# A chunked RWKV-7 recurrence: three chunk inverses side by side on half PSUM banks, their small levels as packed 32x32 squares

## The chip, the cores and the metric

The kernel runs on one core of a Trainium2 chip. TensorE (PE) multiplies into PSUM (8 banks of 128 partitions x 512 fp32), VectorE (DVE) and ScalarE (ACT) read PSUM, GpSimd (POOL) works on SBUF alone, and SyncE (SP) issues most DMAs. The metric is the device time of one execution in microseconds.

## The reference

A decoder trunk of two layers, for one prompt of 16 + 512 positions and eight sample rows of one position, all in fp32. Each layer is `x += ½ FFN(norm x)`, `x += Mixer(norm x)`, `x += ½ FFN(norm x)`. The even layer's mixer has four HGRN2 heads beside eight RWKV-7 heads, the odd layer's has GLA heads. The change touches the RWKV-7 part:

```python
def step(s, inp):                       # rwkv7_scan, per position and head (64 x 64 state)
    rt, wt, kt, vt, kkt, at = inp
    sa = jnp.einsum('bhij,bhj->bhi', s, -kkt)
    s = s * wt[:, :, None, :] + sa[..., None] * (kkt * at)[:, :, None, :] + vt[..., None] * kt[:, :, None, :]
    y = jnp.einsum('bhij,bhj->bhi', s, rt)
    return s, y
...
yn = ((y - mu) * lax.rsqrt(var + RWKV_GN_EPS)).reshape(bsz, t, B_W) * prm['rwkv_ln_w'][e] + prm['rwkv_ln_b'][e]
ob = (yn + bonus.reshape(bsz, t, B_W)) * g
mix = jnp.concatenate([oa.astype(f32), ob], axis=-1).astype(h.dtype) @ prm['even_w_out'][e]
```

## The kernel before

The prompt is cut into one chunk of 16 positions and eight of 64 (`CHUNKS`). Heads go in pairs on 128 partitions, and two such pairs make a group `d`; so there are 2 groups x 9 chunks = 18 units. In a unit the positions of a chunk are coupled by a triangular system, whose inverse is built by doubling: `stage_g` makes the products and the level for blocks of 1, then `lev_t` and `lev_x` for blocks of 2, 4, ... up to half the chunk. `xx` holds the inverse and its transpose, `gm` the masked products, `tm` transposed operands; all three exist for two head pairs side by side. Because the two heads of a pair and two halves of 32 positions lie apart, every level up to 16 is block-diagonal in 32x32 squares, but the kernel before multiplies the full 128x128. The state's update of a unit then goes through `st_p`, `st_t`, `st_sa`, `st_s` and `st_y`, in which PE and a copy or add take turns. `waves` puts all these steps into numbered slots, group 1 later than group 0 by `LAG`, and yields after each step.

`even_mixer` writes out the order of PE by hand (`manual_schedule` for PE; the other engines are ordered by the planner). After each step of the waves it spends a credit, raised by `FILL`, on other work in this order: the HGRN thread `hgrn` (`hproj`, projections in steps of 3 x 272 or 3 x 264 columns, and `hcore`, the recurrence of an HGRN head with `gla_core` and `gla_step`; a core step is charged 2500, for the last head 1000), and, when that is done, the output mix `mix_out` of the first 272 positions. Every `SAMPLE_EVERY` steps it calls the thread of the four RWKV sample states (`rsample`, one after the other; five transposes on PE, then DMA broadcasts, GpSimd products and two reductions; 16 yields each), every `POST_EVERY` steps `post`. `post` goes through the spans of `SPANS`; it starts none until the fourth head's projections are done (`while 3 not in H`), first drains what is left of the sample threads, makes the HGRN norm (`hgrn_norm`) as soon as the HGRN thread is done, and runs `rpost` for two head pairs at a time. The mix may begin when the norm and the spans up to 272 are done. `rsample`, `hgrn_norm` and `rpost` share the two scratch tiles `acc` and `sq`, one buffer each. After the waves:

```python
            now[0] = 10
            for _ in th_:
                pass
            for _ in po:
                if "first" in now and "half" in now:
                    credit = MIX
                    while credit > 0:
                        credit -= next(mo, credit)
            for _ in mo:
                pass
```

PSUM is given out in this stage as rings of whole banks: two for projections (`d`), two of `m` (HGRN cores, sample threads), four of `w` (waves and posts). The lines of the rows below: L240 to L242 projections and mix, L627 and L618 scores of the HGRN cores, L658 their product on GpSimd, L724 and L713 a core's first and last product, L1069 to L1117 the sample thread, L1159 to L1171 `stage_g`, L1182 to L1190 `lev_t`, L1204 and L1206 `lev_x`, L1222 and L1224 `st_p`, L1246 to L1261 `st_s` and `st_y`, L155 with `w` and L1314 to L1328 `rpost`, L176 to L180 and L866 to L869 the HGRN norm.

Of the kernel before, what the change touches and what calls it, by code (L numbers as in the profile page):

```python
# [51 lines left out]
NVEC = _r  # L52


FILL, FILL_MAX = 1100, 5000
CORE, CORE_LAST = 2500, 1000
BESIDE = 2000
AHEAD = 12864
POST = 2000
MIX = 4500  # L60

SAMPLE_EVERY, POST_EVERY = 3, 3
SPANS = [0, 272, 400, 536]
LAG, LAG_LATER = 2, 3
SMALL_BLOCK = 32

HEAD_EVERY, ODD_FILL = 5, 4000
# [2 lines left out]
CU_R, CU_G, CU_END = 0, 6 * 256, 6 * 256 + 6 * 32  # L70
# [36 lines left out]
def trunk(ctx, tc, A, O):  # L107
    nc = tc.nc
    P = 128
    cnt = [0]  # L110

    def til(pool, shape, tag, dt=F32, bufs=None):
        cnt[0] += 1
        kw = {} if bufs is None else {"bufs": bufs}
        return pool.tile(shape, dt, tag=tag, name=f"{tag}_{cnt[0]}", **kw)
# [5 lines left out]
    rings = {}  # L121
    banks = ctx.enter_context(ExitStack())

    def psum(**sizes):
        if sizes == {tag: n for tag, (_, n) in rings.items()}:
            return
        banks.close()
        rings.clear()
        for tag, n in sizes.items():
            pool = banks.enter_context(tc.tile_pool(name=f"ps{tag}", bufs=n, space=bass.MemoryType.PSUM))  # L130
            rings[tag] = (pool, n)

    def bank(tag="m"):
        return til(rings[tag][0], [P, 512], tag)


    cf = til(cst, [P, CF_RM], "cf")
# [983 lines left out]
    def waves(pool, R):  # L1121
# [9 lines left out]
        def lmask(li):  # L1131
            return cu[:, CU_R + 256 * li:CU_R + 256 * li + 256].unsqueeze(1).to_broadcast([P, 2, 256])

        def stage_g(d, ci, U):
            t0, n = CHUNKS[ci]
            na, nl = (2, 32) if n == 64 else (1, n)

            def both(z):  # L1140
                return z.rearrange("p (a h l) -> p a h l", a=2, h=2)[:, :na, :, :nl]

            U["xx"] = til(pool, [P, 2, 256], "xx", bufs=3)
            U["gm"] = til(pool, [P, 2, 320], "gm", bufs=3)
            nc.scalar.copy(U["xx"].rearrange("p u (v c) -> p (u v) c", v=2), ident.unsqueeze(1).to_broadcast([P, 4, P]))
            U["tm"] = til(pool, [P, 2, 384], "tm", bufs=3)
            if n < 64:
                nc.gpsimd.memset(U["gm"], 0.0)
            for i in range(2):
                Q = R[2 * d + i]  # L1150
                b_ = bd[i]
                for h in range(2):
                    hs = slice(64 * h, 64 * h + 64)
                    dst = b_[hs].rearrange("p (v a h l) -> p v a h l", v=4, a=2, h=2)[:, :, :na, h, :nl]
                    nc.vector.tensor_copy(dst, Q["sl"][hs, 0:4, t0:t0 + n].rearrange("p v (a l) -> p v a l", l=nl))
                g = bank("w")
                gv = g[:, 128:384].rearrange("p (v w t) -> p v w t", v=2, w=2)
                rhs = Q["sl"][:, 3:5, t0:t0 + n]
                nc.tensor.matmul(g[:, 0:128], b_[:, 384:512], b_[:, 0:128], start=True, stop=True)  # L1159
                nc.tensor.matmul(gv[:, 0, :, :n], b_[:, 0:128], rhs, start=True, stop=True)  # L1160
                nc.tensor.matmul(gv[:, 1, :, :n], b_[:, 128:256], rhs, start=True, stop=True)
                one = g[:, 128:128 + n].rearrange("p (a l) -> p a l", l=nl)
                nc.vector.tensor_mul(both(U["gm"][:, i, 0:128]), one.unsqueeze(2).to_broadcast([P, na, 2, nl]),
                                     both(maskg[:, 0:128]))
                nc.vector.copy_predicated(U["xx"][:, i, 0:128], cu[:, CU_R:CU_R + 128], g[:, 0:128])
                nc.vector.tensor_mul(*(z.rearrange("p (v t) -> p v t", v=3)[:, :, :n]
                                       for z in (U["gm"][:, i, 128:320], g[:, 192:384], maskg[:, 128:320])))
                pt = bank("w")
                for v in range(3):
                    nc.tensor.transpose(pt[:, 128 * v:128 * v + 128], b_[:, 128 * v:128 * v + 128], ident)  # L1170
                nc.scalar.copy(U["tm"][:, i], pt[:, :384])  # L1171
            nc.vector.copy_predicated(U["xx"][:, :, 128:256], lmask(0)[:, :, 128:256], U["gm"][:, :, 0:128])


        def lev_t(U, li):
            pt = bank("w")
            U["t1"] = til(pool, [P, 2, P], "t1", bufs=2)

            rs, cs = (slice(64, 128), slice(0, 64)) if li == 5 else (slice(0, 128), slice(0, 128))
            ks = cs  # L1180
            for i in range(2):
                nc.tensor.matmul(pt[rs, 128 * i:128 * i + cs.stop], U["gm"][ks, i, rs], U["xx"][ks, i, cs],  # L1182
                                 start=True, stop=True)
            if li > 1:
                px = bank("w")
                for i in range(2):
                    nc.tensor.transpose(px[:, 128 * i:128 * i + 128], U["xx"][:, i, 0:128], ident)  # L1187
            nc.scalar.copy(U["t1"][rs, :, cs], pt[rs, 0:256].rearrange("p (u c) -> p u c", u=2)[:, :, cs])
            if li > 1:
                nc.scalar.copy(U["xx"][:, :, 128:256], px[:, 0:256].rearrange("p (u c) -> p u c", u=2))  # L1190

        def lev_x(U, li, last):
            pd = bank("w")[:, 0:256].rearrange("p (u c) -> p u c", u=2)
            xx, t1 = U["xx"], U["t1"]
            if li == 5:
                a, b = slice(0, 64), slice(64, 128)
                for i in range(2):
                    nc.tensor.matmul(pd[a, i, a], t1[b, i, a], xx[b, i, 192:256], start=True, stop=True)
                nc.vector.tensor_copy(xx[a, :, 192:256], pd[a, :, a])
                return  # L1200
            for i in range(2):
                xt = xx[:, i, 128:256]
                lhsT, rhs = (t1[:, i], xt) if last else (xt, t1[:, i])
                nc.tensor.matmul(pd[:, i], lhsT, rhs, start=True, stop=True)  # L1204
            sl = slice(128, 256) if last else slice(0, 128)
            nc.vector.copy_predicated(xx[:, :, sl], lmask(li)[:, :, sl], pd)  # L1206


        def st_p(d, ci, U):
# [16 lines left out]
        def st_t(d, ci, U):  # L1226
            pt = bank("w")
            for i in range(2):
                nc.tensor.transpose(pt[:, 128 * i:128 * i + 128], pd[d][:, i], ident)
            U["pp"] = til(pool, [P, 2, P], "pp", bufs=2)  # L1230
            nc.scalar.copy(U["pp"], pt[:, 0:256].rearrange("p (u c) -> p u c", u=2))

        def st_sa(d, ci, U):
            ps = bank("w")
            for i in range(2):
                nc.tensor.matmul(ps[:, 128 * i:128 * i + 128], U["xx"][:, i, 128:256], U["pp"][:, i],
                                 start=True, stop=True)
            U["sa"] = til(pool, [P, 2, P], "sa", bufs=2)
            nc.scalar.copy(U["sa"], ps[:, 0:256].rearrange("p (u c) -> p u c", u=2))

        def st_s(d, ci, U):
# [26 lines left out]
        def inverse(d, w, U):  # L1268
            nl = 6 if CHUNKS[w][1] == 64 else 4
            yield lambda: stage_g(d, w, U)  # L1270
            for li in range(1, nl):
                yield lambda li=li: lev_t(U, li)
                yield lambda li=li: lev_x(U, li, li == nl - 1)

        slots = {}
        for d in range(2):
            t = LAG * d
            for w in range(9):
                U = {}
                for fn in inverse(d, w, U):  # L1280
                    slots.setdefault(t, []).append((1 + d, fn, 0))
                    t += 1
                if w == 0 and d == 1:
                    t += LAG_LATER
                for i, st in enumerate((st_p, st_t, st_sa, st_s, st_y)):
                    fn = lambda st=st, d=d, w=w, U=U: st(d, w, U)
                    slots.setdefault(t + i, []).append((0, fn, int(i == 4)))
        ends = 0
        for t in sorted(slots):
            for _, fn, end in sorted(slots[t], key=lambda z: z[0]):  # L1290
# [3 lines left out]
        for d in range(2):  # L1294
            for i in range(2):
                p = 2 * d + i
                ps = bank("w")
                nc.tensor.transpose(ps[:, :P], S[d][:, i], ident)
                so = til(pool, [P, 64], "so", bufs=2)
# [393 lines left out]
```

## Time and profile before

| | |
|---|---|
| median of 3 runs | 2305.53 us (2305.34 to 2306.35) |
| the profiled execution, its own time | 2313.27 us |
| its span from the first to the last instruction | 2311.5 us |
| PE busy | 2256.8 us, 98% |
| VectorE, ScalarE, GpSimd busy | 71%, 47%, 6% |
| PE's granted clock, mean | 0.991 of 2.4 GHz |

Matmuls overlap in PE's pipeline: the duration of one instruction is its way through the array, and what one costs is read from the distance of starts. An fp32 product is two instructions, a transpose is one.

### The profile page before, as it was taken

To read this page: it belongs to the slowest core of one execution; us is meant where nothing else is said; L and a number is where in the kernel's file an instruction comes from. 1 tells how busy PE (TensorE), PEld (TensorE's weight loads), DVE (VectorE), ACT (ScalarE), POOL (GpSimd) and SP (SyncE) were. 2 spreads that over 40 slices of the span, in tenths; PEclk is the share of its full clock that TensorE was granted. 3 is DMA by queue.
4 is the path that set the end of the run, shared out by engine and by line. 5 is a ranking of instruction groups with operands and counts; after the bars stand their busy time and mean duration, and the time that the engine had idled before them with its cause. 6 is when DMAs were issued, how large, how long until landed. Compare 5 with 4: busy or idle time off the path is not lost.

```text
span 2311.5 us, 47443 instructions
## 1 busy us (share of the span) xinstructions
PE 2256.8 (98%) x19520; PEld 2206.5 (95%) x19520; DVE 1646.7 (71%) x2971; ACT 1082.8 (47%) x2056; POOL 143.5 (6%) x192
## 2 busy tenths in 40 slices
PE   8999999999999999999999999999999999999998
PEld 8999999998998888999999999999999889999998
DVE  7858576686666878966757885857666777948576
ACT  6525254374444456434535452525434464525355
POOL 0000000312212100000000000000021210000000
PEclk9999999999999999999999999999999999999999
DMA  6323334223222116242423332333434353333324
GB/s 171 106 78 101 92 92 132 81 64 94 79 71 72 49 49 167 74 119 75 118 74 101 92 110 74 101 92 94 128 110 128 111 160 92 92 92 101 110 85 136
DMA packets 409393, 229.23 MB, mean 99 GB/s; under 512 B 19252, under 2 KB 400501, under 8 KB 409176
## 3 DMA queue, kind: packets, MB, share of 16 engines
q1 hardware_dynamic: 408456, 224.78, 33.5%
q8 instruction: 153, 2.51, 0.5%
q10 hardware_dynamic: 720, 1.42, 0.2%
q14 instruction: 64, 0.52, 0.1%
HBM read 211.19 MB, written 14.97 MB: 98 GB/s over the span
## 4 chain that ended last, share of the span: by engine, by line
PE 86%; DVE 5%; DMA 3%; ACT 2%; issue 1%; POOL 1%; SPq 0%; ACTq 0%; POOLq 0%; DVEq 0%
PE d L334 21%; PE d L335 21%; PE d L336 21%; PE d L240 5%; PE d L242 4%; PE d L241 4%; PE w L1182 1%; PE w L1204 1%; DMA vb<-dv 1%; DVE wlo L229 1%; DMA raw<-in_even_w_out_dram 1%; PE m L155 1%; DMA sq<-dr 1%; DMA raw<-in_odd_w_out_dram 1%; PE w L1187 1%
## 5 line engine op out<-in xcount | busy, mean ns | idle before, releaser
L240 PE MATMUL d<-hh,whi 128*128 128x264 f32 (+2 forms) x1136 | 343.6, 303 | 2.0 <-DVE xT L596 1.3
L242 PE MATMUL d<-hh,wlo 128*128 128x264 f32 (+2 forms) x1136 | 326.7, 288 | 1.9 <-DVE wlo L229 1.7
L241 PE MATMUL d<-hl,whi 128*128 128x264 f32 (+2 forms) x1136 | 326.6, 288 | 0.5 <-DVE hl L1418 0.5
L334 PE MATMUL d<-hh,whi 128*128 128x268 f32 (+1 forms) x832 | 237.8, 286 | 1.8 <-ACT hh L187 1.3
L335 PE MATMUL d<-hl,whi 128*128 128x268 f32 (+1 forms) x832 | 238.1, 286 | 0.9 <-DVE hl L188 0.9
L336 PE MATMUL d<-hh,wlo 128*128 128x268 f32 (+1 forms) x832 | 237.7, 286 | 0.7 <-DVE wlo L293 0.7
L240 PEld LDWEIGHTS d<-hh,whi 128*128 128x128 f32 x1136 | 216.1, 190 | 7.5 <-issue 2.4
L242 PEld LDWEIGHTS d<-hh,wlo 128*128 128x128 f32 x1136 | 215.4, 190 | 4.6 <-DVE wlo L229 4.0
L241 PEld LDWEIGHTS d<-hl,whi 128*128 128x128 f32 x1136 | 216.3, 190 | 0.9 <-DVE hl L1418 0.7
L534 DVE SCALAR_TENSOR_TENSOR xT<-d,xT 128x272 f32<-128x272 f32 (+2 forms) x192 | 82.9, 433 | 166.7 <-PE d L336 166.6
L334 PE MATMUL d<-hid,whi 128*128 128x264 f32 (+2 forms) x704 | 201.5, 287 | 0.0
L334 PE MATMUL d<-hid,whix 128*128 128x264 f32 (+2 forms) x704 | 201.2, 286 | 0.0
L335 PE MATMUL d<-hid,whix 128*128 128x264 f32 (+2 forms) x704 | 200.8, 285 | 0.0
L335 PE MATMUL d<-hid,whi 128*128 128x264 f32 (+2 forms) x704 | 200.7, 286 | 0.0
L336 PE MATMUL d<-hid,wlox 128*128 128x264 f32 (+2 forms) x704 | 200.6, 285 | 0.0
L336 PE MATMUL d<-hid,wlo 128*128 128x264 f32 (+2 forms) x704 | 200.5, 286 | 0.0
L334 PE MATMUL d<-sumh,whix 128*128 128x268 f32 (+1 forms) x576 | 170.9, 297 | 0.0
L336 PE MATMUL d<-sumh,wlo 128*128 128x268 f32 (+1 forms) x576 | 164.7, 286 | 0.0
L335 PE MATMUL d<-suml,whix 128*128 128x268 f32 (+1 forms) x576 | 164.4, 285 | 0.0
L334 PE MATMUL d<-sumh,whi 128*128 128x268 f32 (+1 forms) x576 | 164.2, 285 | 0.0
L336 PE MATMUL d<-sumh,wlox 128*128 128x268 f32 (+1 forms) x576 | 164.0, 285 | 0.0
L335 PE MATMUL d<-suml,whi 128*128 128x268 f32 (+1 forms) x576 | 164.0, 285 | 0.0
(383 smaller groups left out, 6557.8 us busy)
## 6 DMA issues: line engine op xcount, KB each, us to landing
raw<-in_ffn_gate_dram SPq DMA_DIRECT2D x44, 512.0 KB
raw<-in_ffn_up_dram SPq DMA_DIRECT2D x44, 512.0 KB
rawx<-in_ffn_gate_dram SPq DMA_DIRECT2D x44, 512.0 KB
rawx<-in_ffn_up_dram SPq DMA_DIRECT2D x44, 512.0 KB
raw<-in_ffn_down_dram SPq DMA_DIRECT2D x32, 512.0 KB
rawx<-in_ffn_down_dram SPq DMA_DIRECT2D x32, 512.0 KB
raw<-in_even_w_in_dram SPq DMA_DIRECT2D x30, 512.0 KB
raw<-in_odd_w_in_dram SPq DMA_DIRECT2D x25, 512.0 KB
```

The source lines that it names most:

```text
L155: nc.tensor.matmul(ps[:, :b - a], lhsT, rhs[:, a:b], start=True, stop=True)
L229: nc.vector.tensor_sub(lo[:, ks], raw[:, ks], hi[:, ks].bitcast(F32))
L240: nc.tensor.matmul(o, hi[:, k], h, start=(k == 0), stop=False)
L241: nc.tensor.matmul(o, hi[:, k], l, start=False, stop=False)
L242: nc.tensor.matmul(o, lo[:, k], h, start=False, stop=(k == nk - 1))
L334: nc.tensor.matmul(o, hi[:, k], rh(k), start=start and k == 0, stop=False, **kw)
L335: nc.tensor.matmul(o, hi[:, k], rl(k), start=False, stop=False, **kw)
L336: nc.tensor.matmul(o, lo[:, k], rh(k), start=False, stop=stop and k == nk - 1, **kw)
L534: nc.vector.scalar_tensor_tensor(xv[:, sl], ps, -0.5, xv[:, sl], ALU.mult, ALU.add)
L1182: nc.tensor.matmul(pt[rs, 128 * i:128 * i + cs.stop], U["gm"][ks, i, rs], U["xx"][ks, i, cs], start=True, stop=True)
L1187: nc.tensor.transpose(px[:, 128 * i:128 * i + 128], U["xx"][:, i, 0:128], ident)
L1204: nc.tensor.matmul(pd[:, i], lhsT, rhs, start=True, stop=True)
```

## The change

Three inverses run side by side in place of two, each stage of one every third slot (`CHAINS`, `STAGGER`), with the state's steps two slots apart (`OUT_STEP`). A `w` bank is given out as two halves of 256 columns, one after the other. Levels below the last one multiply the four diagonal 32x32 squares of each head pair (`squares_mm`), and `into` spreads the packed result over the masked places of `xx`. In `stage_g` the triangle is made as strips of 32 partitions into the unused part of a bank half, for both head pairs together. The post spans become four, since a half bank holds at most 256 columns. `FILL` falls from 1100 to 550, `SAMPLE_EVERY` goes from 3 to 6, `POST_EVERY` from 3 to 5. `xx`, `gm` and `tm` get four buffers, `pp`, `sa` and `so` one.

```diff
-FILL, FILL_MAX = 1100, 5000
+FILL, FILL_MAX = 550, 5000
...
-SAMPLE_EVERY, POST_EVERY = 3, 3
-SPANS = [0, 272, 400, 536]
-LAG, LAG_LATER = 2, 3
+SAMPLE_EVERY, POST_EVERY = 6, 5
+SPANS = [0, 144, 272, 400, 536]
+CHAINS, STAGGER, OUT_STEP = 3, 4, 2
...
     def bank(tag="m"):
-        return til(rings[tag][0], [P, 512], tag)
+        if tag != "w":
+            return til(rings[tag][0], [P, 512], tag)
+        if not halves:
+            t = til(rings[tag][0], [P, 512], tag)
+            halves.extend((t[:, 256:512], t[:, 0:256]))
+        return halves.pop()
...
-                g = bank("w")
-                gv = g[:, 128:384].rearrange("p (v w t) -> p v w t", v=2, w=2)
+                g, gl = bank("w"), bank("w")
+                gv = g.rearrange("p (v w t) -> p v w t", v=2, w=2)
                 rhs = Q["sl"][:, 3:5, t0:t0 + n]
-                nc.tensor.matmul(g[:, 0:128], b_[:, 384:512], b_[:, 0:128], start=True, stop=True)
+                lt = gl if i == 0 else lt
+                for a in range(na):
+                    for h in range(2):
+                        q = 64 * a + 32 * h
+                        nc.tensor.matmul(lt[q:q + 32, 32 * i:32 * i + nl], b_[:, 384 + q:416 + q],
+                                         Q["sl"][:, 0, t0 + 32 * a:t0 + 32 * a + nl], start=True, stop=True)
...
-                nc.vector.copy_predicated(U["xx"][:, i, 0:128], cu[:, CU_R:CU_R + 128], g[:, 0:128])
...
+                nc.tensor.transpose(gl[:, 128:256], b_[:, 0:128], ident)
                 pt = bank("w")
-                for v in range(3):
-                    nc.tensor.transpose(pt[:, 128 * v:128 * v + 128], b_[:, 128 * v:128 * v + 128], ident)
-                nc.scalar.copy(U["tm"][:, i], pt[:, :384])
+                for v in range(2):
+                    nc.tensor.transpose(pt[:, 128 * v:128 * v + 128], b_[:, 128 * v + 128:128 * v + 256], ident)
+                nc.scalar.copy(U["tm"][:, i, 0:128], gl[:, 128:256])
+                nc.scalar.copy(U["tm"][:, i, 128:384], pt)
+            into(U, 0, lt, 64 * na, nl)
...
+        def into(U, li, ps, rows, nl):
+            src = ps[:rows, 0:64].rearrange("p (u c) -> p u c", u=2)[:, :, :nl]
+            mk = cu[:rows, CU_R + 256 * li:CU_R + 256 * li + 128].rearrange("p (b c) -> p b c", b=4)
+            xx = U["xx"][:rows, :, 0:128].rearrange("p u (b c) -> p u b c", b=4)
+            nc.vector.copy_predicated(xx[:, :, :, :nl], mk.unsqueeze(1).to_broadcast([rows, 2, 4, 32])[:, :, :, :nl],
+                                      src.unsqueeze(2).to_broadcast([rows, 2, 4, nl]))
+        def squares_mm(ps, lhs, rhs):
+            for i in range(2):
+                for q in range(0, P, 32):
+                    nc.tensor.matmul(ps[q:q + 32, 32 * i:32 * i + 32], lhs[:, i, q:q + 32], rhs(i, q),
+                                     start=True, stop=True)
...
+                U["t1"] = til(pool, [P, 2, 32], "t1c", bufs=CHAINS)
+                squares_mm(pt, U["gm"], lambda i, q: U["xx"][:, i, q:q + 32])
...
+            if not last:
+                squares_mm(ps, xx[:, :, 128:256], lambda i, q: t1[:, i])
+                into(U, li, ps, P, 32)
+                return
...
+        free = [STAGGER * i for i in range(CHAINS)]
+        after, ends = [0, 0], []
+        for c in range(18):
+            d, w, U = c % 2, c // 2, {}
+            k = free.index(min(free))
+            t = max(free[k], ends[c - CHAINS - 1] if c > CHAINS else 0)
+            for fn in inverse(d, w, U):
+                slots.setdefault(t, []).append((1 + k, fn, 0))
+                t += CHAINS
+            free[k] = t
+            t = max(t - CHAINS + 2, after[d])
+            for i, st in enumerate((st_p, st_t, st_sa, st_s, st_y)):
+                fn = lambda st=st, d=d, w=w, U=U: st(d, w, U)
+                slots.setdefault(t + OUT_STEP * i, []).append((0, fn, int(i == 4)))
+            after[d] = t + 4 * OUT_STEP
+            ends.append(after[d])
```

## Rows read from the trace of the kernel before

**Rows 1.** The page: busy time by engine, and the chain that ended last.
```profile
PE 2256.8 (98%) x19520; PEld 2206.5 (95%) x19520; DVE 1646.7 (71%) x2971; ACT 1082.8 (47%) x2056; POOL 143.5 (6%) x192
...
PE 86%; DVE 5%; DMA 3%; ACT 2%; issue 1%; POOL 1%; SPq 0%; ACTq 0%; POOLq 0%; DVEq 0%
```
**Rows 2.** Windows of the stage: stretch, length, busy us by engine (instructions), PE clock, DMA.
```profile
520.30:868.70 348.40, 328.69 (x3406) 306.97 (x3405) 243.82 (x708) 160.92 (x437) 68.82 (x72) 0.98 0.24 69
868.70:889.80 21.10, 20.43 (x163) 20.19 (x164) 16.73 (x45) 10.51 (x29) 0.00 (x0) 1.00 0.43 121
```
**Rows 3.** Timeline of PE (start us, us, what): the fourth head's core begins and ends.
```profile
777.51 0.27 PE L724 MATMUL m<-cf,hv 128*8 128x128 f32 x1
...
816.39 0.39 PE L713 MATMUL m<-hq,S 128*128 128x128 f32 x2
```
**Rows 4.** Timeline: the fourth sample thread's first transposes, first GpSimd product, last reduction.
```profile
699.64 0.27 PE L1069 MATMUL m<-cf,sl 128*8 128x128 f32 x1
...
716.36 1.47 POOL L1091 TENSOR_TENSOR sq<-acc,sq 128x512 f32<-128x512 f32 x1
...
742.09 0.69 DVE L1117 TENSOR_REDUCE sl<-sq 128x8 f32<-128x512 f32 x1 [2.40 <-POOL sq L1115]
```
**Rows 5.** Timeline of PE: full products, and a step of projection between two of them.
```profile
645.99 0.39 PE L1246 MATMUL w<-tm 128*128 128x128 f32 x2
...
646.88 0.61 PE L1204 MATMUL w<-t,xx 128*128 128x128 f32 x4
647.25 0.37 PE L240 MATMUL d<-hh,whi 128*128 128x272 f32 x1
...
647.71 0.61 PE L1182 MATMUL w<-xx,gm 128*128 128x128 f32 x4
```
**Rows 6.** Timeline of PE: 32-wide score products, 64x64 products, and what follows each.
```profile
549.75 0.46 PE L627 MATMUL m<-hq,hk 128*32 128x32 f32 x32
550.14 0.38 PE L1236 MATMUL w<-pp,xx 128*128 128x128 f32 x1
...
653.45 0.44 PE L1198 MATMUL w<-xx,t 64*64 64x64 f32 x4
653.82 0.39 PE L240 MATMUL d<-hh,whi 128*128 128x264 f32 x1
```
**Rows 7.** Groups by line and form, PE, 520.3 to 868.7: count | busy us, mean ns | idle before.
```profile
L1182 PE MATMUL w<-xx,gm 128*128 128x128 f32 x280 | 45.0, 284 | 1.9 <-DVE xx L1206 1.9
L1204 PE MATMUL w<-t,xx 128*128 128x128 f32 x272 | 43.2, 283 | 1.3 <-ACT xx L1190 0.6 <-ACT t L1188 0.5
```
**Rows 8.** Groups by line and form, VectorE and ScalarE, 510 to 875: readers of `w`.
```profile
L1206 DVE COPY_PREDICATED xx<-cu,w 128x256 f32<-128x256 uint8 x70 | 30.5, 439 | 19.0 <-PE w L1204 18.4
...
L1166 DVE TENSOR_TENSOR gm<-w,cf 128x192 f32<-128x192 f32 x32 | 11.1, 347 | 0.0
...
L1163 DVE TENSOR_TENSOR gm<-w,cf 128x128 f32<-128x128 f32 x32 | 9.1, 284 | 4.6 <-PE w L1161 4.2
...
L1239 ACT COPY sa<-w 128x256 f32<-128x256 f32 x18 | 6.7, 373 | 4.6 <-PE w L1236 4.4
```
**Rows 9.** The same view: two engines that read one bank in `st_p`.
```profile
L1222 DVE COPY pd<-w 64x128 f32<-64x128 f32 x18 | 5.3, 295 | 13.0 <-ACT pd L1222 12.8
...
L1224 ACT COPY py<-w 128x128 f32<-128x128 f32 x18 | 4.7, 262 | 6.3 <-DVE pd L1222 6.3
```
**Rows 10.** The same view, GpSimd: a core's level.
```profile
L658 POOL TENSOR_TENSOR hk<-hk,dlev 128x264 f32<-128x264 f32 x12 | 10.8, 898 | 20.6 <-PE m L638 12.2 <-issue 8.0 <-POOL vb L750 0.4
```
**Rows 11.** Timeline: the norm's first and last work, a pair of posts' first and last.
```profile
828.30 0.65 ACT L176 ACTIVATE acc<-oa 128x536 f32<-128x536 f32 x1 [0.43 <-DVE hl L1328]
...
846.74 0.77 DVE L869 SCALAR_TENSOR_TENSOR hl<-oa,vcol,hh 128x536 fp32r<-128x536 f32 x1
...
868.30 0.29 DVE L1314 SCALAR_TENSOR_TENSOR acc<-w,sl 128x136 f32<-128x136 f32 x1
...
877.19 0.30 DVE L1328 TENSOR_TENSOR hl<-sq,hh 128x136 fp32r<-128x136 f32 x1 [0.16 <-ACT hh L1327]
```

More of the change, by code (lines that the diff above doesn't have):

```diff
@@ L126, in psum @@
             return
+        halves.clear()
         banks.close()
@@ L131, in psum @@
             rings[tag] = (pool, n)
+    halves = []
     def bank(tag="m"):
-        return til(rings[tag][0], [P, 512], tag)
+        if tag != "w":
[4 more added lines that the diff above has]
+        return halves.pop()
     cf = til(cst, [P, CF_RM], "cf")
@@ L1141, in both @@
                 return z.rearrange("p (a h l) -> p a h l", a=2, h=2)[:, :na, :, :nl]
-            U["xx"] = til(pool, [P, 2, 256], "xx", bufs=3)
-            U["gm"] = til(pool, [P, 2, 320], "gm", bufs=3)
+            U["xx"] = til(pool, [P, 2, 256], "xx", bufs=CHAINS + 1)
+            U["gm"] = til(pool, [P, 2, 320], "gm", bufs=CHAINS + 1)
             nc.scalar.copy(U["xx"].rearrange("p u (v c) -> p (u v) c", v=2), ident.unsqueeze(1).to_broadcast([P, 4, P]))
-            U["tm"] = til(pool, [P, 2, 384], "tm", bufs=3)
+            U["tm"] = til(pool, [P, 2, 384], "tm", bufs=CHAINS + 1)
             if n < 64:
@@ L1160, in stage_g @@
+                for a in range(na):
[3 more added lines that the diff above has]
+                                         Q["sl"][:, 0, t0 + 32 * a:t0 + 32 * a + nl], start=True, stop=True)
                 nc.tensor.matmul(gv[:, 0, :, :n], b_[:, 0:128], rhs, start=True, stop=True)
                 nc.tensor.matmul(gv[:, 1, :, :n], b_[:, 128:256], rhs, start=True, stop=True)
-                one = g[:, 128:128 + n].rearrange("p (a l) -> p a l", l=nl)
+                one = g[:, 0:n].rearrange("p (a l) -> p a l", l=nl)
@@ L1163, in stage_g @@
                 nc.vector.tensor_mul(both(U["gm"][:, i, 0:128]), one.unsqueeze(2).to_broadcast([P, na, 2, nl]),
                                      both(maskg[:, 0:128]))
-                nc.vector.copy_predicated(U["xx"][:, i, 0:128], cu[:, CU_R:CU_R + 128], g[:, 0:128])
                 nc.vector.tensor_mul(*(z.rearrange("p (v t) -> p v t", v=3)[:, :, :n]
-                                       for z in (U["gm"][:, i, 128:320], g[:, 192:384], maskg[:, 128:320])))
+                                       for z in (U["gm"][:, i, 128:320], g[:, 64:256], maskg[:, 128:320])))
@@ L1168, in stage_g @@
+                nc.tensor.transpose(gl[:, 128:256], b_[:, 0:128], ident)
                 pt = bank("w")
-                for v in range(3):
-                    nc.tensor.transpose(pt[:, 128 * v:128 * v + 128], b_[:, 128 * v:128 * v + 128], ident)
-                nc.scalar.copy(U["tm"][:, i], pt[:, :384])
-            nc.vector.copy_predicated(U["xx"][:, :, 128:256], lmask(0)[:, :, 128:256], U["gm"][:, :, 0:128])
-        def lev_t(U, li):
-            pt = bank("w")
[L1177 to L1183, printed above, removed]
+                for v in range(2):
+                    nc.tensor.transpose(pt[:, 128 * v:128 * v + 128], b_[:, 128 * v + 128:128 * v + 256], ident)
@@ new lines, in squares_mm, with lev_t @@
+        def squares_mm(ps, lhs, rhs):
[3 more added lines that the diff above has]
+                                     start=True, stop=True)
+        def lev_t(U, li, last):
+            pt = bank("w")
+            if last:
+                U["t1"] = til(pool, [P, 2, P], "t1", bufs=2)
+                rs, cs = (slice(64, 128), slice(0, 64)) if li == 5 else (slice(0, 128), slice(0, 128))
+                ks = cs
+                for i in range(2):
+                    nc.tensor.matmul(pt[rs, 128 * i:128 * i + cs.stop], U["gm"][ks, i, rs], U["xx"][ks, i, cs],
+                                     start=True, stop=True)
+            else:
+                U["t1"] = til(pool, [P, 2, 32], "t1c", bufs=CHAINS)
+                squares_mm(pt, U["gm"], lambda i, q: U["xx"][:, i, q:q + 32])
@@ L1187, in lev_t @@
                     nc.tensor.transpose(px[:, 128 * i:128 * i + 128], U["xx"][:, i, 0:128], ident)
-            nc.scalar.copy(U["t1"][rs, :, cs], pt[rs, 0:256].rearrange("p (u c) -> p u c", u=2)[:, :, cs])
+            if last:
+                nc.scalar.copy(U["t1"][rs, :, cs], pt[rs, 0:256].rearrange("p (u c) -> p u c", u=2)[:, :, cs])
+            else:
+                nc.scalar.copy(U["t1"], pt[:, 0:64].rearrange("p (u c) -> p u c", u=2))
             if li > 1:
@@ L1192, in lev_x @@
         def lev_x(U, li, last):
-            pd = bank("w")[:, 0:256].rearrange("p (u c) -> p u c", u=2)
+            ps = bank("w")
+            pd = ps[:, 0:256].rearrange("p (u c) -> p u c", u=2)
             xx, t1 = U["xx"], U["t1"]
@@ L1200, in lev_x @@
                 return
+            if not last:
+                squares_mm(ps, xx[:, :, 128:256], lambda i, q: t1[:, i])
+                into(U, li, ps, P, 32)
+                return
             for i in range(2):
[L1202 to L1206, printed above, removed]
+                nc.tensor.matmul(pd[:, i], t1[:, i], xx[:, i, 128:256], start=True, stop=True)
+            nc.vector.copy_predicated(xx[:, :, 128:256], lmask(li)[:, :, 128:256], pd)
         def st_p(d, ci, U):
@@ L1229, in st_t @@
                 nc.tensor.transpose(pt[:, 128 * i:128 * i + 128], pd[d][:, i], ident)
-            U["pp"] = til(pool, [P, 2, P], "pp", bufs=2)
+            U["pp"] = til(pool, [P, 2, P], "pp", bufs=1)
             nc.scalar.copy(U["pp"], pt[:, 0:256].rearrange("p (u c) -> p u c", u=2))
@@ L1237, in st_sa @@
                                  start=True, stop=True)
-            U["sa"] = til(pool, [P, 2, P], "sa", bufs=2)
+            U["sa"] = til(pool, [P, 2, P], "sa", bufs=1)
             nc.scalar.copy(U["sa"], ps[:, 0:256].rearrange("p (u c) -> p u c", u=2))
@@ L1271, in inverse @@
             for li in range(1, nl):
-                yield lambda li=li: lev_t(U, li)
+                yield lambda li=li: lev_t(U, li, li == nl - 1)
                 yield lambda li=li: lev_x(U, li, li == nl - 1)
         slots = {}
[L1276 to L1287, printed above, removed]
+        free = [STAGGER * i for i in range(CHAINS)]
[14 more added lines that the diff above has]
+            ends.append(after[d])
         ends = 0
@@ L1298, in waves @@
                 nc.tensor.transpose(ps[:, :P], S[d][:, i], ident)
-                so = til(pool, [P, 64], "so", bufs=2)
+                so = til(pool, [P, 64], "so", bufs=1)
                 for h in range(2):
```

## The prediction

> **What bounds the kernel now.** The page comes first: TensorE (PE) is busy 98% of the span, and the chain that ended last runs through PE for 86% of it [rows 1]. So the question is what the change does to PE's work and to PE's waits in the stage it touches. The windows cut that stage in two: from the first wave product to the last, 348.4 us, and then the rest of the posts beside the output mix, 21.1 us. PE is idle for 19.7 and 0.7 us of them, 20.4 in all, and its clock is granted at 0.98 and 1.00 of 2.4 GHz [rows 2]. VectorE is busy 70% of the first stretch and bounds nothing by itself.
>
> The order of PE is written out, so I followed it on paper. The 18 inverses give 16 x 11 + 2 x 7 = 190 steps and the state updates 18 x 5 = 90: 280 steps. After each, FILL units of credit buy other PE work. The HGRN thread is the first in line: 141,504 columns of projections and 48 core steps (36 at 2,500, 12 at 1,000), 243,500 units. With 1,100 a step the waves earn 313,000, so that thread ends inside them, at step 236 by my count once the posts' charges are taken off. The trace agrees: the last core starts at 777.51 and its last product is at 816.39, 85% into the waves [rows 2, 3]. The fourth sample thread starts at 699.64 [rows 4], and two of the three post spans are done before the waves end. All that waits on slow chains is thus covered by wave products.
>
> **The change part by part.** *Squares.* A level up to 16 tokens below the last loses two 128x128 products (four instructions) at each of its two stages and gets eight 32x32 ones (16 instructions). The eight instructions from 645.99 to 646.88 took 0.11 us each, so four take 0.45 [rows 5]. 32 small ones of the scores take 0.39 us up to the next start, the drain behind them included; before them the pipe drains for some 0.1 [rows 6]. Sixteen therefore take about 0.35 us. Bounds: 0.24 us (no drains) and, by columns, the rate of the 64x64 products, four with 64 columns in 0.37 us [rows 6], so sixteen with 32 columns in 0.74. I take 0.35, the nearest row by shape. There are 136 such stages: the 272 instructions each of L1182 and L1204 [rows 7], by four (eight 128-wide ones of L1182 stay). They save 14 us; the 36 triangular products made as four strips each lose some 2. **-12 us** (+40 to -27). The Trainium skill, page "TensorE: Matmul & The Clock Gate", section "Wait — 56ns, not 53.3ns?", says that start-to-start never drops below about 25 ns. By that sixteen would take 0.40 and the drains, a loss of about 20 us instead; the 32 in 0.39 us contradict it for four column strips, and no row shows squares on four row groups.
>
> ScalarE's and VectorE's copies shrink or stay, off PE's path. Fewer buffers for pp and sa cost nothing: by the slot order their next writer comes after the last reader, and what lies between covers it; otherwise a wait of one read, 0.37 us [rows 8], in each of 18 chunks, 7 us, inside the range.
>
> *Half banks.* Two takers in a row now share a bank. Does a PE write wait for the other half's reader? No row shows PE in that place. The nearest: ScalarE's copy of py (L1224) reads other columns than VectorE's copy of pd (L1222) and waits for it 6.3 us in total, and the VectorE copy waits 12.8 us for a ScalarE copy of other partitions of the same bank [rows 9]. So engines are kept apart by bank, whatever the columns, and I take the wait as real. The Trainium skill, page "PSUM — Partial Sum Buffer", section "PSUM bank collisions raise a hardware error", says the same of a PE write against a reader at disjoint columns of a bank: it must be guarded by bank. No run so far shows that for PE, and the sum does not rest on it.
>
> Its price: in the first stage of an inverse the transpose into gl shares a bank with g (17 of 36 times) and must wait for the two products that VectorE reads from g: 0.28 + 0.35 us [rows 8] and a PE latency of 0.27 (a product's own duration) [rows 4], less its own 0.11, some 0.85 us. The second block's triangle goes into the first block's gl, which ScalarE is still copying out, some 0.65. That is 1.5 us for each of 18, **27 us**. By the written order 139 further pairs join different steps of which the second follows the first directly; 85 have no fill between and 54 have a step of projection, 0.46 us [rows 5]. A reader needs 0.27 of latency and 0.37 to 0.44 of work [rows 8]: 0.5 us lost for the 85, 0.1 for the 54, **48 us**. Sum **+75 us**; the lower end is 35 (half of the reads already done), the upper 110 (queues ahead of the readers).
>
> *Half the fill.* With 550 a step the 280 steps earn 159,000: 94,100 columns of projection and 26 core steps. When the waves end, ten steps of the third head's core, all of the fourth head's, and 47,400 columns of its projections are left. No post can have begun, since each waits for the fourth head's projections. The sample threads are called every 6th step, 47 times of the 64 needed, so the fourth has not started. After the waves the program drains these one after the other in PE's order:
> - The third core beside the projections: about full. The fourth alone: seven levels, each a GpSimd product (0.90 us) [rows 10], scores and PE latency of 0.7 us, 1.7 in all, then copies and states: some 20 us for 10 of PE work (six groups of scores at 0.48 with their drains, some 64 other instructions at 0.11). **+10** (5 to 15).
> - The fourth sample thread, of which PE does only five transposes: 699.64 to 742.78 us before, 43 us; from its first GpSimd product at 716.36 it is a chain of transfers and products, 26.4 us [rows 4]. It ran beside other work, so 36. It holds the two scratch tiles that the norm and every post need. **+36** (27 to 43).
> - The HGRN norm, 828.30 to 847.5 beside waves [rows 11], alone some 14, with almost no PE work: **+13** (10 to 18).
> - Spans 0 to 144 and 144 to 272: no mix is allowed before they end. A pair of posts took 868.30 to 877.49, 9.2 us, with VectorE also serving the mix [rows 11]; alone I estimate 7.5, with PE work of 1. Four pairs: **+26** (22 to 34).
> - The last two spans beside the mix: four pairs at the 10.3 us that the last two pairs before took on average in their 21.1 us [rows 2], 41, for some 25 of mix (64 steps, together at somewhat less than the 0.46 of a lone one) and 4 of posts: **+12** (8 to 18).
>
> Of the 20.4 us of idle time before, what the two remaining heads cause in the waves stays, some 6: **-14** (0 to -20).
>
> **Sum.** -12 - 14 + 75 + 10 + 36 + 13 + 26 + 12 = +146 us. The profiled execution took 2313.27 with a span of 2311.5; the median shown is 2305.53, so I add to that: **2451 us**. The terms' ends together, without the dear squares, give +75 to +226.
>
> **The rivals.**
> *The halves cost nothing* (chance 0.14): PE writes one half while the other is read. For it: no row shows PE waiting so; against it: the two copies that keep apart by bank [rows 9]. +71, 2376 us.
> *The squares are dear* (0.08): at the rate of the 64x64 products they lose 38 us instead of saving 14. For it: drains at each change of shape; against it: the scores' 32 in 0.39. 2451 + 52 = 2503 us. By the 25 ns floor that the Trainium skill's page "TensorE: Matmul & The Clock Gate" states it would be some 2485.
> *PE stays the bound in any order* (0.04): whatever PE comes to has been read or made by then, because the three inverses and the scratch work leave the other engines time ahead. For it: VectorE has 30% to spare in the waves, and sample chain, norm and posts need little of PE; against it: the shared scratch tiles, and PE's written order, in which the first PE instructions of the fourth sample thread and of all posts stand behind the last core. The time is then PE's work alone, -12 and some 10 of the idle time gone: 2283 us, faster. It decides at PE's idle time in the two stretches, 20.4 us before: faster only while that stays under 32.
> *No difference* (0.02): single terms cancel.
> The forecast itself, waits for banks and an uncovered end, has 0.72.
>
> **How the numbers follow.** 2451 is the likeliest case. The range, 2370 to 2505, reaches to the free halves below and the dear squares above, and leaves out the faster case and the corners. A change under 0.2%, about 5 us, counts as none, about what a measurement of this kernel can tell. Faster 0.04, same 0.02, slower 0.94.
>
> **What would show it.** The fourth group of the five sample transposes stands behind the last head's last product, with PE idle after it for 27 us or more; the first post's reciprocal comes after the last wave; the stretch of waves is shorter than 348.4 us, with PE idle there for 40 us or more, named as waits for ScalarE and VectorE reads of w at the products after the first half; sixteen squares take about 0.35 us. Wrong: the fourth sample thread done before the waves end, no idle time at the second halves, or squares above 0.5 us.

## The result and the profile after

The changed kernel takes 2539.26 us, the median of four runs, and the kernel before 2305.94 us beside it: a ratio of 1.101 (95% interval 1.0971 to 1.1049), 233 us slower. The four runs lie between 2533.74 and 2547.01, so a difference of up to some 13 us from a single run of another version shows nothing. The direction was forecast. The size was not: 2451 us, with a range that ended at 2505.

The profiled execution of the changed kernel took 2533.74 us, with a span of 2531.9. On its page, three lines answer to [rows 1]: busy time by engine, the granted clock in 40 slices, and the chain that ended last by engine.

```profile
PE 2331.4 (92%) x21384; PEld 2227.7 (88%) x21384; DVE 1661.0 (66%) x2989; ACT 1086.6 (43%) x2104; POOL 139.1 (5%) x192
...
PEclk9999999978998975599999999999999999999999
...
PE 54%; DVE 3%; DMA 2%; ACT 1%; issue 1%; POOL 1%; SPq 0%; ACTq 0%; POOLq 0%; DVEq 0%
```

TensorE (PE) is busy 92% of the span instead of 98%, but for longer: 2331 us instead of 2257. A page on which PE only waited more would show the same busy time. The second line says what else happened: the clock is 0.9 or more in most slices and lower in six of the nine from about 505 to 1,075 us, between 0.5 and 0.6 in two of them.

The windows cut that stage at its seams: the waves; what is left of the HGRN heads, the fourth core included; the fourth sample thread and the start of the norm; the rest of the norm and the posts, the last of them beside the mix; the first stretch of work behind them. Columns as in [rows 2].

```profile
520.60:897.40 376.80, 301.77 (x4436) 241.65 (x4436) 173.29 (x508) 126.73 (x399) 44.13 (x48) 0.86 0.14 41
897.40:978.00 80.60, 60.87 (x678) 55.92 (x678) 36.73 (x97) 15.05 (x38) 11.66 (x17) 0.67 0.19 53
978.00:1020.60 42.60, 1.44 (x7) 0.48 (x4) 4.58 (x7) 4.20 (x7) 8.39 (x7) 0.50 0.31 95
1020.60:1112.00 91.40, 64.46 (x361) 55.82 (x362) 65.69 (x168) 31.53 (x78) 0.00 (x0) 0.75 0.16 46
1112.00:1180.00 68.00, 62.59 (x467) 60.69 (x467) 55.23 (x95) 34.17 (x54) 0.00 (x0) 0.95 0.45 125
```

The stage that ended at 889.8 before now ends at 1112. These 222 us are the whole difference of the spans, 220.4. Over the first four rows PE is busy 428.5 us, where [rows 2] add up to 349.1: +79. It is idle for 162.9 us (75.0, 19.7, 41.2, 26.9) where it was idle for 20.4: +142. So a third of the loss is longer busy time of PE, which the prediction had 12 us *shorter*.

PE's waits in the waves (who waits, for whom, us in total, times, longest):

```profile
PE w L1183 <- DVE gm L1181: 12.7, 18, 1.1
PE w L1204 <- ACT py L1266: 8.3, 9, 1.7
PE w L1174 <- ACT tm L1188: 5.7, 9, 0.6
PE w L1204 <- ACT xx L1230: 4.5, 11, 0.5
```

L1183 is the transpose into `gl`, L1181 VectorE's read of `g`, the other half of the same bank: one wait in each of the 18 units, where 17 were forecast. L1174 are the triangle strips of the second block, written into the first block's `gl`; they wait for ScalarE's copy out of `pt` (L1188), which in 9 units is the other half of that bank. The two places come to 18.4 us, where 27 were forecast. L1204 are the squares in a half whose other half is being read. The Trainium skill, page "PSUM — Partial Sum Buffer", section "PSUM bank collisions raise a hardware error", asks for such a guard between a PE write and a reader of other columns of a bank. The trace agrees in that the program has this wait, 12.7 us at L1183; no run shows what the chip would do without it.

The squares themselves, on PE's timeline (start us, us, line, operation, count), once at full clock and once at half:

```profile
686.73 0.33 PE L1204 MATMUL w<-t1c,xx 128*32 128x32 f32 x16
686.99 0.39 PE L251 MATMUL d<-hh,whi 128*128 128x264 f32 x1
...
700.61 0.44 PE L1204 MATMUL w<-t1c,xx 128*32 128x32 f32 x16
700.99 0.60 PE L251 MATMUL d<-hh,whi 128*128 128x272 f32 x1
```

The sixteen instructions (x16) are the eight products of one stage. They take 0.26 us to the next start; with the drain ahead of them, some 0.1, that is the 0.35 of the prediction. Their form, `128*32 128x32`, says how they lie: each result is a 32x32 square, but the product reaches over all 128 partitions and has weights of 32 columns, one of four column strips by the 32 partitions of its result. That is the form of the score products in [rows 6]. By the Trainium skill's floor of about 25 ns from start to start (page "TensorE: Matmul & The Clock Gate", section "Wait — 56ns, not 53.3ns?") sixteen would take an estimated 0.40 us. The trace contradicts that for products that take turns on four column strips, with 0.26. In the second pair the squares take 0.38 and the projection behind them 0.60 instead of 0.39 us: the same instructions at 1.2 instead of 2.4 GHz.

After the waves, the fourth sample thread, on the same timeline:

```profile
977.65 0.63 PE L724 MATMUL m<-hq,S 128*128 128x128 f32 x2
978.08 0.42 PE L1080 MATMUL m<-cf,sl 128*8 128x128 f32 x1
...
978.50 0.94 PE L1080 MATMUL m<-cf,sl 128*8 128x128 f32 x3
1020.62 0.82 PE L166 MATMUL m<-acc,cf 128*128 128x272 f32 x1 [41.17 <-DVE acc L191]
```

The transposes stand behind the last product of the last core, and PE is then idle for 41.17 us. Some 36 of them go to the thread's chain of transfers, GpSimd products and VectorE work. Its last reduction and the norm's first work on the freed scratch tile start together, on the timeline of VectorE and ScalarE:

```profile
1015.58 0.65 ACT L187 ACTIVATE acc<-oa 128x536 f32<-128x536 f32 x1 [33.76 <-POOL sq L1126]
1015.58 0.69 DVE L1128 TENSOR_REDUCE sl<-sq 128x8 f32<-128x512 f32 x1 [22.86 <-POOL sq L1126]
```

The last 5 us are squares and sums of the norm, up to the VectorE sum (L191) that releases PE.

### The profile page after: what moved, and what is told of

Its sections match the earlier page's. It is cut to its first block, busy times and chain, and to the rows that moved or that the text cites. A ratio compares the mean times of both kernels' runs of the same rounds, so it can differ in the third digit from the quotient of the medians.

```text
span 2531.9 us, 51231 instructions
## 1 busy us (share of the span) xinstructions
PE 2331.4 (92%) x21384; PEld 2227.7 (88%) x21384; DVE 1661.0 (66%) x2989; ACT 1086.6 (43%) x2104; POOL 139.1 (5%) x192
## 4 chain that ended last, share of the span: by engine, by line
PE 54%; DVE 3%; DMA 2%; ACT 1%; issue 1%; POOL 1%; SPq 0%; ACTq 0%; POOLq 0%; DVEq 0%
PE d L345 15%; PE d L347 14%; PE d L346 14%; PE d L251 3%; PE d L253 2%; PE d L252 2%; PE w L166 1%; DMA vb<-dv 1%; DMA raw<-in_odd_w_out_dram 0%; DMA sq<-dr 0%; DVE sl L1365 0%; PE m L166 0%; DMA raw<-in_even_w_out_dram 0%; DVE wlo L240 0%; PE m L747 0%
## 5 line engine op out<-in xcount | busy, mean ns | idle before, releaser
L251 PE MATMUL d<-hh,whi 128*128 128x264 f32 (+2 forms) x1136 | 349.0, 308 | 4.6 <-ACT whi L239 2.4
```

What stands on the lines that cost most here:

```text
L251: nc.tensor.matmul(o, hi[:, k], h, start=(k == 0), stop=False)
```

## The experiments

The explanation to be tested, theory 1: the waits cost about what was forecast, and besides, a PE that waits often is granted a lower clock, which stretches the work between the waits. The rivals were that the squares stretch PE's work by themselves, that the slots cost, and that the pace only moves work that PE does anyway. Times without an interval are of one execution each, the profiled one; medians of the kernel before beside them lay between 2304.72 and 2307.39.

**Pace and halves, each undone, and both.** One kernel gets the old pace, one whole `w` banks, one both:

```diff
-FILL, FILL_MAX = 550, 5000
+FILL, FILL_MAX = 1100, 5000
...
-SAMPLE_EVERY, POST_EVERY = 6, 5
+SAMPLE_EVERY, POST_EVERY = 3, 3
```

```diff
-        if tag != "w":
-            return til(rings[tag][0], [P, 512], tag)
-
-        if not halves:
-            t = til(rings[tag][0], [P, 512], tag)
-            halves.extend((t[:, 256:512], t[:, 0:256]))
-        return halves.pop()
+        t = til(rings[tag][0], [P, 512], tag)
+        return t if tag != "w" else t[:, 0:256]
```

> The changed kernel with the old pace (FILL 1100, sample every 3rd step, posts every 3rd), half banks kept. Theory (PE stands for half banks and for the uncovered end, and its granted clock then falls, which stretches the work it has): the end is covered again, so the 88 us of idle time behind the waves and the slow clock there go; the waits for banks stay at 50 to 75 us with the clock at about 0.9: 2350 to 2375 us. Rival (the squares and their changes of shape themselves stretch PE's work, whatever PE waits for): PE's work in the stage stays some 50 us above that of before and the bank waits come on top: 2390 us or more.

> The changed kernel with a whole bank for every taker of w, slow pace kept. Theory: the waves lose their 74 us of idle time, the clock there is above 0.95 and they take 255 to 275 us in place of 377; the end behind them stays about 215 us at a low clock: 2415 to 2435 us. Rival: without any waits for banks the waves still take over 310 us, since the squares stretch PE's work: 2470 us or more.

> Both undone: whole banks and the old pace, with squares, three inverses side by side and four spans kept. Theory: clock about 0.98 or more, PE's idle time 20 us or less, squares save 12 us: 2285 to 2305 us. Rival: the squares cost PE time by themselves, so this is slower than the kernel before by 20 us or more.

Old pace: 2477.92 us. Whole banks: 2387.71. Both: 2324.2, a ratio of 1.0081 (1.0065 to 1.0098) to before. The expectation for the pace missed by over 100 us, the one for the banks by 27 the other way: the halves are worth more than either said. For both undone, theory 1 missed too: 2324.2 is 19 us above the end of its range and just short of the rival's 20 us over the kernel before. The effects add up: the halves cost 2539.3 - 2387.7 = 152 us at the slow pace and 2477.9 - 2324.2 = 154 at the old one; the slow pace costs 61 with halves and 64 without; 19 remain. The kernel with whole banks, its windows at the same seams:

```profile
520.00:789.00 269.00, 253.51 (x4436) 213.44 (x4433) 173.12 (x508) 125.39 (x397) 44.73 (x48) 0.97 0.20 56
789.00:857.00 68.00, 52.16 (x678) 47.66 (x677) 36.35 (x98) 15.63 (x40) 11.47 (x17) 0.78 0.23 65
857.00:897.50 40.50, 1.03 (x6) 0.41 (x4) 4.58 (x7) 4.20 (x7) 8.39 (x7) 0.54 0.34 100
897.50:973.30 75.80, 58.05 (x344) 53.48 (x344) 60.69 (x159) 29.91 (x77) 0.00 (x0) 0.77 0.17 49
```

In the waves the same 4,436 PE instructions are busy for 253.51 us at a clock of 0.97, where the halves made them 301.77 at 0.86. Of the 107.8 us that the halves add there, 59.5 are idle time (75.0 less 15.5) and 48.3 are longer busy time. How much of that is the clock can be counted, since the clock has two levels, 2.4 and 1.2 GHz, and the trace tells when each was granted. Over the stretches at 1.2 GHz inside these waves the windows add up to this, first with halves, then with whole banks:

```profile
sum 107.84, PE 92.31 PEld 74.68 DVE 42.44 ACT 26.10 POOL 18.58; mean PE 10.26 PEld 8.30 DVE 4.72 ACT 2.90 POOL 2.06
```

```profile
sum 13.65, PE 13.34 PEld 11.57 DVE 7.05 ACT 2.77 POOL 2.53; mean PE 4.45 PEld 3.86 DVE 2.35 ACT 0.92 POOL 0.84
```

PE is busy for 92.3 us at the lower level instead of 13.3. Half of the difference, some 40 us, is what the lower clock adds; the source of the other 9 is not told apart. The work after the waves, sample thread left out, is 15.1 us busier too with halves (60.87 + 64.46 against 52.16 + 58.05, with 17 instructions more), and takes 28 us longer.

**The pace on the kernel before.** `FILL` 550, `SAMPLE_EVERY` 6, `POST_EVERY` 5 and nothing else.

> The kernel before with nothing but the slow pace (FILL 550, sample every 6th step, posts every 5th). Theory: the waves take about 265 us, then come the rest of the HGRN thread, the fourth sample thread, the norm and the posts one after the other with a low clock, as in the changed kernel, about 190 to 215 us: 2390 to 2415 us. Rival (the pace only moves work that PE does anyway): within 20 us of the kernel before.

2398.26 us, 93 more than the 2304.93 beside it, inside what was expected. This is the uncovered end by itself, with full products and whole banks:

```profile
520.00:806.00 286.00, 264.04 (x2605) 247.79 (x2604) 171.23 (x522) 129.59 (x363) 45.13 (x47) 0.98 0.19 53
...
873.70:914.70 41.00, 1.37 (x6) 0.47 (x4) 4.58 (x7) 4.18 (x7) 8.39 (x7) 0.54 0.34 99
914.70:983.00 68.30, 53.04 (x314) 46.30 (x314) 57.65 (x127) 28.03 (x65) 0.00 (x0) 0.84 0.18 54
```

The sample thread and the start of the norm take their 41 us here as well, whatever the inverses look like.

**Squares and slots, each alone.** Three kernels: the changed one with the old pace, spans and slots and with whole banks, so that the squares, the new first stage and the buffer counts are left; the one before with the new slots and buffer counts alone; and the one before with squares in the levels alone, first stage untouched. From the last one's edit:

```diff
-                nc.tensor.matmul(pt[rs, 128 * i:128 * i + cs.stop], U["gm"][ks, i, rs], U["xx"][ks, i, cs],
-                                 start=True, stop=True)
...
+                squares_mm(pt, U["gm"], lambda i, q: U["xx"][:, i, q:q + 32])
...
+            if not last:
+                squares_mm(ps, xx[:, :, 128:256], lambda i, q: t1[:, i])
+                into(U, li, ps, P, 32)
+                return
```

> The kernel before with the squares alone: whole banks, old pace, old slots (two groups side by side), three spans. The run with whole banks and the old pace took 2324 us, 19 more than before, with PE idle only 27 us but its clock at 0.95. Theory 1 (squares take PE time away, but keep it so lightly used that its clock falls): the clock is below that of before (0.97 or less in the waves) and the time is 2310 to 2330 us. Theory 2 (squares are a plain gain, the 19 us come from the slots with three side by side): 2288 to 2300 us, clock 0.98 as before.

> The kernel before with the new slots alone (three inverses side by side, state steps two slots apart, four buffers), full products, whole banks, old pace, three spans. Theory 1 (the clock is lost to the squares): within 8 us of the kernel before, clock 0.98 in the waves. Theory 2 (the slots with three side by side cost): 2315 to 2335 us.

> The kernel before with squares in the levels alone: first stage, slots, whole banks, pace and spans as before. Squares alone with the new first stage took 2311 us, 7 more than before. Theory 1 (the new first stage, with six banks and PE waiting there, ate the 14 us that the squares save): 2290 to 2299 us, faster than before. Theory 2 (drains and a lower clock take back what squares save): 2302 to 2314 us.

Squares with the new first stage: 2311.39, ratio 1.0031 (1.0017 to 1.0045). Slots: 2313.32, 1.0042 (1.0027 to 1.0057). Squares in the levels: 2309.64, 1.000 (0.9984 to 1.0016). None gains: the theory held for the first, the rival for the last, and the slots came out between the two. The last one's waves, in the window of [rows 2]:

```profile
520.30:868.70 348.40, 322.60 (x5041) 279.86 (x5039) 243.10 (x708) 152.76 (x438) 67.78 (x72) 0.96 0.25 69
```

PE's busy time falls by 6.1 us from 328.69 and its idle time rises by as much; the clock is 0.96 instead of 0.98. Counted by clock level as above, PE is busy for 28.6 us at 1.2 GHz instead of 15.4, which takes some 7 us. At full clock its work is thus 12.7 us less, nearly the 14 that the squares were to save. The whole executions point the same way: the mean clocks of the twelve lie between 0.987 and 0.992, those of the kernel before beside them between 0.989 and 0.995.

**Does the clock carry the stretched work, or does the work only look longer beside the waits?** If waits lower the clock, work of no use to anyone, put into the waits, must make the kernel faster. That needs a bank that nobody reads, so a control has three `w` banks and a spare one, and the test puts one product ahead of each second half (`FILLERS` is 1):

```diff
-        psum(d=2, m=2, w=4)
+        psum(d=2, m=2, w=3, j=1)
...
+        elif "j" in rings:
+            if not spare:
+                spare.append(til(rings["j"][0], [P, 512], "j"))
+            for _ in range(FILLERS):
+                nc.tensor.matmul(spare[0][:, 0:128], ident, ident, start=True, stop=True)
```

> The changed kernel with three banks for w (six halves) in place of four, the fourth set aside. It is the control for the next run. Every reader is awaited one bank earlier: 2540 to 2580 us.

> The control with one idle product of 128x128 (0.22 us at full clock, some 250 of them, 55 us of added PE work in all) on the spare bank just before the first write of every second half, where PE waits for the other half's reader. Theory (PE waits there and its clock falls because of it): the products run inside the waits, PE's idle time in the waves drops by 35 us or more, the granted clock there rises above 0.93, and the time falls by 15 us or more against the control although work was added. Rival (PE's work is dear for itself, the clock follows something else): the time grows by 30 us or more.

Control 2555.29 us, with fillers 2521.61: 34 us faster with 506 instructions more, and 12 us under the fastest run of the changed kernel. PE's idle time in the waves falls from 73.6 to 50.6 us, by less than the 35 expected. The waves of the control, and then of the kernel with fillers:

```profile
520.00:926.80 406.80, 333.25 (x4439) 268.27 (x4438) 175.01 (x508) 126.96 (x399) 43.62 (x48) 0.76 0.13 38
```

```profile
520.00:897.40 377.40, 326.78 (x4866) 275.35 (x4866) 175.01 (x507) 126.32 (x399) 44.40 (x48) 0.97 0.14 40
```

With fillers the clock is 0.97 instead of 0.76, and PE is busy for 6.5 us less although it runs 427 instructions more. At 0.11 us each (a full product in [rows 5]) the fillers are 47 us of that, so the other work takes some 280 instead of 333. A rival in which only the waits are longer has no place for that.

How far the clock falls is another matter. The control was to wait more than the changed kernel, and it doesn't: 73.6 us of idle time in the waves against 75.0, and its first wait is the same as above:

```profile
PE w L1183 <- DVE gm L1181: 12.5, 18, 1.1
```

Yet its clock there is 0.76 against 0.86, and its waves take 30 us more. So waits of the same length do not fix the clock. The four runs of the changed kernel show it too: mean clocks of 0.946 and 0.947 go with 2533.74 and 2533.96 us, 0.939 twice with 2544.55 and 2547.01. Part of the 34 us may be this spread. The clock in the waves lies outside it: 0.97 with fillers, and 0.76 to 0.86 in the four profiles with halves at this pace and no fillers (the changed kernel, the control and the next two runs).

**The sample threads earlier.** The changed kernel with `SAMPLE_EVERY` 3 alone, so that the fourth thread starts inside the waves.

> The changed kernel with the sample threads called every 3rd step again, nothing else. All four are then done inside the waves. Theory (the fourth sample thread stands by itself behind the waves, 42 us in which PE has nothing): its 41 us of idle time go and the work after it runs at a better clock: 2475 to 2500 us. Rival (what follows needs that time anyway, the norm and the posts wait for VectorE and ScalarE): 2520 us or more.

2505.47 us, 34 less than the changed kernel's median and 28 less than its profiled execution; 5 us above the expected range, below the rival's. Its waves, the thread's five transposes among them:

```profile
520.00:911.00 391.00, 313.84 (x4443) 252.47 (x4441) 174.79 (x514) 128.23 (x403) 52.49 (x55) 0.82 0.16 44
```

The stretch of 42.6 us behind the core is gone, and the waves take 14 us more, 12 of them busy time of PE at a clock of 0.82.

**One bank wait taken away.** The transpose into `gl` ahead of VectorE's reads of `g`:

```diff
+                nc.tensor.transpose(gl[:, 128:256], b_[:, 0:128], ident)
                 one = g[:, 0:n].rearrange("p (a l) -> p a l", l=nl)
...
-                nc.tensor.transpose(gl[:, 128:256], b_[:, 0:128], ident)
```

> The changed kernel with one line moved: the transpose into gl is issued before VectorE reads g, so that it has no reader of its bank to wait for. Theory (each wait for the other half costs its own length and again some of it through the clock): the 12.7 us of waits named there go and the time falls by 15 to 35 us, to 2505 to 2525. Rival (the next PE write of the stage waits for the same engines in its place): within 8 us of the changed kernel.

2535.39 us, 4 less than the median and inside the changed kernel's own spread: the rival held. PE's waits in its waves:

```profile
PE w L1174 <- ACT tm L1187: 9.2, 9, 2.9
PE w L1204 <- ACT py L1266: 7.4, 9, 1.7
PE w L1174 <- ACT tm L1188: 5.7, 9, 0.6
```

The 12.7 us at the transpose are gone, and 9.2 us stand at the strips (L1174), which wait for ScalarE's copy out of the first block's `gl`, the half that they write (L1187). Up to the end of its waves, at 903.7 us, PE is idle for 71.9 us where it was 75.0. Here, taking one reader's wait away moved it to the next.

## Why the prediction was wrong

The direction, the places of the waits that the prediction named and their causes were right. Step by step:

- *Half banks, +75 us:* the step that failed. They cost 152 us. The idle part was sized well: 59.5 us in the waves, inside the bounds of 35 to 110. Of its parts, the 0.85 us at the transpose come to 0.79 when added up, and the trace has 0.71 a unit (12.7 us over 18). What it left out is that PE's work was taken at one duration whatever the waits. Between the waits the same instructions ran at a granted clock of 0.86 instead of 0.97 and were busy for 48 us more in the waves alone, some 40 of them by the clock; what is left of the 152 lies mostly behind the waves, where the clock is lower too. The fillers show that filling idle time brings the clock back. How low it falls for given waits stays open.
- *Squares, -12 us:* the stage came out at its 0.35 us, but the sum did not. That no row shows squares on four row groups was a misreading: the scores of [rows 6] have the very form of the squares. In the levels alone the squares gain nothing (1.000). At full clock they save 12.7 us of PE's work; the lower clock takes some 7 of them back and idle time 6. Why the clock and the idle time change is not settled; a shorter product may leave the readers less cover. Squares, new first stage, slots and spans together cost 19 us where the sum had them gain 12; the slots alone, which had no term in it, are 9 of that, the squares with the first stage 7.
- *Half the fill, +97 us, less 14 of idle time filled:* 61 to 64 on the changed kernel, 93 on the one before. The named parts hold in place and order, and the first post's reciprocal (L1365) starts at 1031.7, behind the waves. The thread takes some 36 us of idle PE, as forecast, the start of the norm 5 more. Norm and posts take 96 us (5 + 91.4), where the terms were worked out from 14 + 30 + 41 = 85. The core leaves PE idle for 19.7 us instead of 10. The estimate was 20 us high for the changed kernel and 10 low for the one before; which of its terms carries that isn't told apart, since the end is stretched by the clock (0.67 and 0.75) as well.
- *Together:* 19 + 63 + 152 = 234, measured 233. This closes by construction, as the three are steps from one kernel to the other; what is measured is that halves and pace cost about the same in either order. Against the sum of +146 the halves were 77 too low, squares and slots 31, the pace 20 too high: 88, the miss. The range was also narrower than its own terms: their upper ends add up to +226, some 2532 us, and it stopped at 2505.
- *Waves shorter than 348.4 us:* wrong with halves, 376.8; right with whole banks, 269.
- *The rivals:* free halves fall by the whole-bank kernel (152 us); dear squares by the 0.26 us on the timeline; PE as the bound in any order by 163 us of idle time in the four stretches.

The Trainium skill describes a case near the missing step, on its page "TensorE: Matmul & The Clock Gate", section "A second HAM failure mode: psum-queue depth-cycling": in a kernel measured there, short idle times of PE between groups of products, where it cycles through banks, made the clock swing. The trace agrees: waits of at most 1.7 us, most of them at bank halves, and a clock of 0.86 that goes back and forth between the two levels.

None of the versions beats the kernel before; the squares in the levels equal it.

## What to carry to other kernels

When a change makes a busy TensorE wait, price the wait twice: once as idle time, and once as the clock that the work beside it may lose; here that was 60 us and some 40 us in the waves. And compare single runs of such a kernel with care, since its clock differs from run to run. Give two products that follow one another different banks when other engines read them, and look at PE's idle time and clock before work that is saved is counted as time. What a lower fill saves inside the waves must find cover behind them: put the starts of long chains ahead of the last wave. That was tried for the sample thread (28 to 34 us), not for the norm.

## What was unexpected of the hardware

The clock fell to 0.86 and 0.76 on average in the waves of the changed kernel and of the control, whose idle time there, 75.0 of 376.8 us and 73.6 of 406.8, is made of waits of at most 1.7 us. Products of no use in these gaps raised it to 0.97, and the kernel took 34 us less than the control and 12 less than the fastest run of the changed kernel. With the same waits the clock was 0.86 in one kernel and 0.76 in the other. And sixteen instructions with weights of 128x32, in turn on the four column strips of the array, took 0.26 us up to the next start, 16 ns each.
